# A two-layer decoder trunk on one core: all splits of the expert blocks on DVE, gathered tokens' pairs among the dense gates, 24 instead of 34 blocks in plain fp32

## The chip, the core and the metric

One core of a Trainium2 chip runs the whole step. Its engines are TensorE (PE, with its weight loads PEld), VectorE (DVE), ScalarE (ACT), GpSimd (POOL) and SyncE (SP, which here only issues DMAs). Each engine works through its own instructions strictly in order; semaphores tie the engines together. The metric is device microseconds of one execution, lower is better. A block below is one 128x1024 fp32 tile of an expert table, 512 KB.

## The reference

Each of the two layers runs a mixer (layer 0: gated linear attention and RG-LRU; layer 1: RWKV-7) and then PEER, a retrieval over 16384 one-neuron experts. The change lies in PEER alone:

```python
def block(xb):                       # 128 tokens
    q = normalised (xb @ w_q) per head
    s1, s2 = q[..., :128] @ keys0.T, q[..., 128:] @ keys1.T
    v1, i1 = lax.top_k(s1, 16); v2, i2 = lax.top_k(s2, 16)
    cand = v1[..., :, None] + v2[..., None, :]
    sc, pos = lax.top_k(cand.reshape(..., 256), 16)
    eidx = (i1 * 128 + i2) at pos
    gate = jax.nn.softmax(sc)
    act = jax.nn.gelu(u_tab[eidx] . xb)
    return sum(gate * act * v_tab[eidx])
```

There are 304 tokens: 16 learned ones, 256 of a prompt and 32 of samples.

## The kernel before

`peer` (L738) works in two ways. For 256 tokens it is **dense**: all 128 blocks of the table u go through PE (`up`), the gelu of each block is multiplied by a gate matrix that is zero except at the chosen experts (`weigh`, L1015), and all 128 blocks of v are accumulated into PSUM (`down`). The other tokens (48 in layer 0, 32 in layer 1) are **gathered**: POOL issues indirect DMAs for their rows of u and v (`rows`, L1073) and DVE does the dot products (`gup`, L1080) and the weighted sum (`gdown`, L1094). Layer 0 has 24 gathers of u and 24 of v, layer 1 has 16 and 16, each of two 512 KB DMAs, through three buffers `ab`.

Most blocks run as three fp32r products instead of one fp32 product, for which a block is **split**: ACT rounds raw into `wh` (L170), and DVE or POOL subtracts `wl = raw - wh` (L171). `wh` and `wl` have 3 buffers each, `raw` has 5. `u_pool` and `v_pool` (L202 and L203) say which blocks POOL subtracts: u blocks 34 to 59 and the odd ones above, every fifth v block below 100 and every second one from 100 on, 94 of 222 per layer. The first `nf` = 34 u blocks are not split; they run as plain fp32 (16 matmul instructions each) against `x32`.

The stages of one layer are: queries and top 16; `pairs(0)`, which ranks the 256 dense tokens' candidates; the **gate stage**, in which 32 calls of `ggroup` build the gate matrix (DVE writes one-hot tiles into the three buffers `ab`, PE multiplies them, ACT copies, SP writes 1 MB to the DRAM tensor `G` after every second call) while PE also runs the u blocks up to `ahead` = 36; then the **dense stage**, from the first `down` to the last, in which one v block and one u block alternate for 92 steps and v blocks alone follow for 36. Every eighth `weigh` loads 1 MB of `G` back into a `gb` buffer. `pairs(1)` and `gprep` rank the gathered tokens' candidates and work out their rows; the gathers start 100 units after `tp`.

The order is made by due times: `at(due, fn)` collects all units, they are traced in order of `due`, and a scheduler that goes by its own estimates then orders the instructions on each engine. `late` additionally keeps a unit's instructions behind the last marked instruction of the same engine. The units are estimated microseconds; `tw` is the due time of the first `down`, `tu` = 2.56 is one block.

Of the kernel before, what the change touches and what calls it, by code (L numbers as in the profile page):

```python
# [20 lines left out]
P = 128  # L21
# [147 lines left out]
def split(nc, src, h, l, eng=None):  # L169
    nc.scalar.activation(h, src, AF.Copy)  # L170
    return (eng or nc.vector).tensor_tensor(l, src, f(h), op=ALU.subtract)  # L171
# [10 lines left out]
class Prog:  # L182
    def __init__(self, tc, a, es):
        self.tc, self.nc, self.a, self.es = tc, tc.nc, a, es
        self.n, self.mark, self.turn, self.ready = 0, {}, {}, []
        self.extra(None, 0, 0)
        pool = lambda name, **kw: es.enter_context(tc.tile_pool(name=name, **kw))
        self.const = pool("const", bufs=1)
        self.strm = pool("strm", bufs=1)
        self.xp = pool("xp", bufs=1)  # L190
        self.ps = pool("ps", bufs=1, space=PSUM)
        k = self.const.tile([P, 4 * P], F32, name="k_all")
        self.k = k
        self.ident, self.o1024, self.o256, self.iota = (k[:, j * P:(j + 1) * P] for j in range(4))
        self.kdiag = self.const.tile([P, 48], F32, name="k_diag")
        pp = dict(ring=42, ahead=36, nf=34, lag=14, g2=-50, tq=10.0, ps=91.0, pl=42.0, gs=2.85, gl=14.0, u0=78.0, us1=3.5,
                  um=60, vm=5, te=25, vt=100, wu=0, wv=0, cl=0.01, us=2, gj=0.5)
        self.pp = pp
        self.mp = dict(q0=-3.6, q1=.12, p0=-3.0, p1=.14, a0=-2.2, a1=.14, i0=-1.45, i1=.2, c0=0, c1=.24, t0=1.5, t1=.15,
                       o0=.2774, o1=.1, f0=-1.0, f1=4.0, fe=.15, f2=7.9085, fl=.035)  # L200
        self.ring, self.lag, self.g2 = (pp[n] for n in ("ring", "lag", "g2"))
        self.u_pool = lambda e: e < pp["um"] or e % pp["us"] == 1  # L202
        self.v_pool = lambda e: e % (pp["vm"] if e < pp["vt"] else 2) == 0  # L203
        self.mhalf = self.const.tile([P, 6], F32, name="mhalf")
        self.nc.gpsimd.memset(self.mhalf, -0.5)
        self.vm1 = self.const.tile([P, 13, KB], F32, name="vm1")
        self.shf = self.const.tile([P, KB, 8], F32, name="shf")
        self.lnv = self.const.tile([P, 8, KB], F32, name="lnv")
# [529 lines left out]
    def peer(self, xh, xl, l):  # L738


        nc, a = self.nc, self.a
# [5 lines left out]
        with ExitStack() as es:  # L747
            pp = es.enter_context(self.tc.tile_pool(name=f"pe{l}", bufs=1, reuse_waits="tile"))
# [5 lines left out]
            gb = lambda shape, dt=F32: self.t(pr, shape, dt, "gb", 4)  # L754
            G = self.t(dp, [16, P, P, 16], F32, "G")
# [3 lines left out]
            at = lambda due, fn, *args: units.append((due, len(units), fn, args))  # L759

            def late(due, fn, *args):

                def queued():
                    with ExitStack() as q:
                        for ins in self.mark.values():
                            q.enter_context(self.tc.issue_after(getattr(ins, "ins", ins)))
                        fn(*args)
                at(due, queued)
# [171 lines left out]
            gs = [None]  # L940
# [24 lines left out]
            pp_ = self.pp  # L965
# [3 lines left out]

            wts = {}  # L970

            def up_load(e):
                if e < pp_["nf"]:
                    raw = self.stream("raw", F32)
                    nc.sync.dma_start(raw, a[f"ut{l}"][e])
                    wts["u", e] = raw, None
                    return
                wts["u", e] = self.wtile(a[f"ut{l}"][e], nc.gpsimd if self.u_pool(e) else None)

            def up(e):  # L980
                wh, wl = wts.pop(("u", e))
# [11 lines left out]
            gr, coef = [None], {}  # L993

            def down_load(e):
                hl = gb([P, 2, KB, P], F32R) if e == P - 1 else None
                wts["v", e] = self.wtile(a[f"v{l}"][e * P:(e + 1) * P, :].rearrange("p (k d) -> p k d", k=KB),
                                         nc.gpsimd if self.v_pool(e) else None, hl if hl is None else (hl[:, 0], hl[:, 1]))

            def weigh(e):  # L1000

                if e % 8 == 0:
                    gr[0] = gb([P, 16, 8, 16])
                    nc.sync.dma_start(gr[0].rearrange("p b i t -> p b (i t)"),
                                      G[:, :, e:e + 8, :].rearrange("b p i t -> p b (i t)"))
                if e >= P - NL:
                    ch, cl = (tl([P, 256], "act", NR, F32R) for _ in range(2))
                elif e % 2:
                    cc = tl([P, 2, 256], "qs", 3, F32R)
                    ch, cl = cc[:, 0, :], cc[:, 1, :]  # L1010
                else:
                    ch, cl = (tl([P, 256], "sc", 6, F32R) for _ in range(2))
                c = acts.pop(e)
                v16 = lambda ap: ap.rearrange("p (b t) -> p b t", t=16)
                self.mark[True] = nc.vector.tensor_tensor(v16(c), v16(c), gr[0][:, :, e % 8, :], op=ALU.mult)  # L1015
                split(nc, c, ch, cl)
                coef[e] = ch, cl
# [95 lines left out]
            tq, tu = pp_["tq"], 2.56  # L1113
# [8 lines left out]
            for h in range(8):  # L1122
                t, z = tq * h, h == 7
# [4 lines left out]
                b = t + (12.5 if z else 23.3)  # L1128
# [4 lines left out]
            ps = pp_["ps"]  # L1133
            at(ps, pairs_now, 0)
            tg = ps + pp_["pl"]
# [2 lines left out]
            for q in range(32):  # L1138
                at(tg + 1 + pp_["gs"] * q, ggroup, q)
            tw = tg + 1 + 32 * pp_["gs"] + pp_["gl"]  # L1140
            tp = tw + self.g2

            steps = pairs(1)
            for j in range(14):
                (at if j < 10 else late)(tw - pp_["gl"] + 0.5 + 0.8 * j if j < 10 else tp + 42 + 3 * j, lambda: steps.pop(0)())
            late(tp + 85, gprep)
            ahead, u0, u1 = pp_["ahead"], pp_["u0"], pp_["us1"]
            n0 = int((tg - u0) / u1)
            for e in range(P):
                if e < n0:  # L1150
                    tup = u0 + u1 * e
                elif e < ahead:
                    tup = tg + (tw - tg) * (e - n0 + 0.5) / (ahead - n0)
                else:
                    tup = tw + 2 * tu * (e - ahead) + 0.1
                tdn = tw + 2 * tu * e if e < P - ahead else tw + 2 * tu * (P - ahead) + tu * (e - P + ahead)
                at(tup - pp_["wu"], up_load, e)
                at(tup, up, e)
                at(tdn - (pp_["wv"] if e else 4.0), down_load, e)
                at(tdn - pp_["cl"], weigh, e)  # L1160
                at(tdn, down, e)
            gc = [(g, c) for g in range(len(groups)) for c in range(0, groups[g][1], 2)]
            t1 = tp + 100
            te = tw + 2 * tu * (P - ahead) + tu * ahead
            tg = (te - pp_["te"] - 15 - t1) / (2 * len(gc))
            for j, (g, c) in enumerate(gc):
# [626 lines left out]
```

## Time and profile before

| what | us |
| --- | --- |
| median of 3 runs | 2682.76 (2682.07 to 2689.53) |
| profiled execution | 2687.88 |
| its span, first to last instruction | 2686.1 |
| gate stage, layer 0, to the first `down` | 360 to 498 |
| dense stage, layer 0 | 498 to 1178 |
| dense stage, layer 1 | 1989 to 2650 |

The two dense stages are half of the span. PE is busy for 2478 us and its weight loads for 2259 us; POOL is busy for 1063 us, DVE for 1906 us. A busy PE is not yet PE at its pace: its granted clock has two levels (1.2 and 2.4 GHz), and the profile gives the mean of a stretch as a share of the higher one. Idle time of an engine counts only where another engine waits for it, so the way to read this profile is by stage: how long PE idles there, at which clock it works, and on whom it waits.

### The profile page before, as it was taken

The numbers are of one execution on the slowest core, as the hardware profiler recorded it, in microseconds if no ns is written. First come the engines' busy times: TensorE is split into PE (matmuls) and PEld (weight loads), VectorE is DVE, ScalarE is ACT, GpSimd is POOL, SyncE is SP. The second block draws the span as 40 slices with busy tenths as digits, with TensorE's granted clock in tenths as the row PEclk, the third lists the DMA queues.
The fourth block names the chain that finished last, engine by engine and source line by source line (L and its number), as shares of the span: only waits on it lengthen the run. The fifth ranks groups of instructions, "written<-read, shape, count | busy, mean of one in ns | idle before, by whom it ended". The sixth has DMA issues, their size and how long they took to land. (4 is left out here: it accounts for less than half of the span.)

```text
span 2686.1 us, 46850 instructions
## 1 busy us (share of the span) xinstructions
PE 2478.1 (92%) x18242; PEld 2258.7 (84%) x18242; DVE 1905.8 (71%) x4002; ACT 1146.9 (43%) x2072; POOL 1063.3 (40%) x836
## 2 busy tenths in 40 slices
PE   7999999989999999978999998899998899999996
PEld 6878889879999999977666656787997899999996
DVE  5455886568676888768587785589657766677776
ACT  7424233434444444434454452433343444444443
POOL 3335100356444454556333432520034534444444
PEclk9979999999999999988999999899999999999998
DMA  5323345687777988642211102324577767797772
GB/s 160 102 76 120 95 173 213 203 262 263 264 270 260 364 275 299 230 136 80 68 41 41 35 24 97 107 91 154 213 226 233 236 236 236 241 319 263 264 237 92
DMA packets 197895, 490.08 MB, mean 182 GB/s; under 512 B 21397, under 2 KB 91429, under 8 KB 192937
## 3 DMA queue, kind: packets, MB, share of 16 engines
q1 hardware_dynamic: 173480, 401.10, 45.7%
q0 software_dynamic: 23040, 83.90, 8.5%
q8 instruction: 143, 2.34, 0.4%
q10 hardware_dynamic: 1152, 2.10, 0.2%
q14 instruction: 80, 0.65, 0.1%
HBM read 447.41 MB, written 39.63 MB: 181 GB/s over the span
## 5 line engine op out<-in xcount | busy, mean ns | idle before, releaser
L171 POOL TENSOR_TENSOR wl<-raw,wh 128x1024 fp32r<-128x1024 f32 x240 | 615.1, 2565 | 1103.0 <-ACT wh L170 1055.0
L170 ACT ACTIVATE wh<-raw 128x1024 fp32r<-128x1024 f32 x519 | 549.0, 1059 | 813.2 <-PE ps_mm L162 362.5
L171 DVE TENSOR_TENSOR wl<-raw,wh 128x1024 fp32r<-128x1024 f32 x279 | 364.5, 1307 | 171.3 <-ACT wh L170 163.4
L162 PE MATMUL ps_u<-xh,wl 128*128 128x256 f32 x1504 | 427.0, 284 | 17.7 <-DVE wl L171 10.2
L162 PE MATMUL ps_u<-xh,wh 128*128 128x256 f32 x1504 | 428.5, 285 | 0.0
L162 PE MATMUL ps_u<-xl,wh 128*128 128x256 f32 x1504 | 425.3, 283 | 0.0
L162 PE MATMUL ps_mm<-qs,wh 128*128 128x256 f32 x1984 | 373.0, 288 | 0.0
L162 PE MATMUL ps_mm<-sc,wh 128*128 128x256 f32 x1984 | 358.3, 282 | 6.8 <-DVE sc L171 3.6
L162 PEld LDWEIGHTS ps_mm<-qs,wh 128*128 128x128 f32 x1984 | 315.7, 195 | 1.1 <-issue 0.8
L162 PE MATMUL ps_mm<-qs,wl 128*128 128x256 f32 x992 | 287.3, 290 | 31.6 <-DVE wl L171 31.6
L162 PEld LDWEIGHTS ps_mm<-sc,wh 128*128 128x128 f32 x1984 | 308.8, 193 | 8.2 <-DVE sc L171 4.2
L162 PEld LDWEIGHTS ps_u<-xh,wl 128*128 128x128 f32 x1504 | 287.2, 191 | 20.2 <-DVE wl L171 11.2
L162 PE MATMUL ps_mm<-sc,wl 128*128 128x256 f32 x992 | 279.9, 283 | 16.7 <-DVE wl L171 15.6
L162 PEld LDWEIGHTS ps_u<-xh,wh 128*128 128x128 f32 x1504 | 287.9, 191 | 0.1
L162 PEld LDWEIGHTS ps_u<-xl,wh 128*128 128x128 f32 x1504 | 287.5, 191 | 0.1
L1015 DVE TENSOR_TENSOR act<-act,gb 128x256 f32<-128x256 f32 x256 | 153.7, 642 | 114.0 <-DMA gb<-G 107.5
L162 PEld LDWEIGHTS ps_mm<-qs,wl 128*128 128x128 f32 x992 | 194.2, 196 | 34.8 <-DVE wl L171 34.0
L162 PEld LDWEIGHTS ps_mm<-sc,wl 128*128 128x128 f32 x992 | 191.3, 193 | 18.3 <-DVE wl L171 16.6
L171 DVE TENSOR_TENSOR sc<-act,sc 128x256 fp32r<-128x256 f32 x124 | 171.1, 1380 | 50.0 <-ACT sc L170 50.0
L990 ACT ACTIVATE act<-ps_u 128x256 f32<-128x256 f32 x256 | 94.8, 371 | 153.4 <-PE ps_u L162 153.4
L162 PE MATMUL ps_u<-wh,raw 128*128 128x256 f32 x544 | 140.1, 389 | 9.0 <-ACT act L990 9.0
L162 PE MATMUL ps_mm<-xh,wh 128*128 128x304 f32 x416 | 134.7, 327 | 8.6 <-ACT xh L344 4.2
(556 smaller groups left out, 4926.9 us busy)
## 6 DMA issues: line engine op xcount, KB each, us to landing
raw<-in_ut SPq DMA_DIRECT2D x256, 512.0 KB
raw<-in_v SPq DMA_DIRECT2D x256, 512.0 KB
G<-gb SPq DMA_DIRECT2D x32, 1024.0 KB
gb<-G SPq DMA_DIRECT2D x32, 1024.0 KB
raw<-in_wq SPq DMA_DIRECT2D x32, 512.0 KB
raw<-in_w_in SPq DMA_DIRECT2D x20, 512.0 KB
raw<-in_w_out SPq DMA_DIRECT2D x8, 512.0 KB
raw<-in_w_r SPq DMA_DIRECT2D x8, 512.0 KB
```

The costliest lines, as they stand in the source:

```text
L162: nc.tensor.matmul(out, lhsT, rhs, start=start, stop=stop, skip_group_check=True)
L170: nc.scalar.activation(h, src, AF.Copy)
L171: return (eng or nc.vector).tensor_tensor(l, src, f(h), op=ALU.subtract)
L990: nc.scalar.activation(acts[e], pu, AF.Gelu_apprx_tanh)
L1015: self.mark[True] = nc.vector.tensor_tensor(v16(c), v16(c), gr[0][:, :, e % 8, :], op=ALU.mult)
```

## The change

`u_pool` and `v_pool` are gone: `wtile` is called without an engine, and DVE subtracts all 104 split u blocks and 128 v blocks of each layer. `nf` falls from 34 to 24. The loads of `G` become a unit of their own, `gates_load`, due four blocks ahead of the `weigh` that needs them. `pairs(1)` and `gprep` are traced among the calls of `ggroup`, and no longer as `late` units in the dense stage. The gathers start 15 units after `tw` (before: 50 after it), and `lag`, from a gather to the arithmetic on it, is 20 instead of 14 units.

```diff
-        pp = dict(ring=42, ahead=36, nf=34, lag=14, g2=-50, tq=10.0, ps=91.0, pl=42.0, gs=2.85, gl=14.0, u0=78.0, us1=3.5,
-                  um=60, vm=5, te=25, vt=100, wu=0, wv=0, cl=0.01, us=2, gj=0.5)
+        pp = dict(ring=42, ahead=36, nf=24, lag=20, g2=15, tq=10.0, ps=91.0, pl=42.0, gs=2.85, gl=14.0, u0=78.0, us1=3.5,
+                  te=25, wu=0, wv=0, cl=0.01, gj=0.5)
-        self.u_pool = lambda e: e < pp["um"] or e % pp["us"] == 1
-        self.v_pool = lambda e: e % (pp["vm"] if e < pp["vt"] else 2) == 0
...
-                wts["u", e] = self.wtile(a[f"ut{l}"][e], nc.gpsimd if self.u_pool(e) else None)
+                wts["u", e] = self.wtile(a[f"ut{l}"][e])
...
-                                         nc.gpsimd if self.v_pool(e) else None, hl if hl is None else (hl[:, 0], hl[:, 1]))
+                                         None, hl if hl is None else (hl[:, 0], hl[:, 1]))
+            def gates_load(e):
+                gr.append(gb([P, 16, 8, 16]))
+                nc.sync.dma_start(gr[-1].rearrange("p b i t -> p b (i t)"),
+                                  G[:, :, e:e + 8, :].rearrange("b p i t -> p b (i t)"))
...
                 if e % 8 == 0:
-                    gr[0] = gb([P, 16, 8, 16])
-                    nc.sync.dma_start(gr[0].rearrange("p b i t -> p b (i t)"),
-                                      G[:, :, e:e + 8, :].rearrange("b p i t -> p b (i t)"))
+                    gr[0] = gr.pop(1)
...
-            tp = tw + self.g2
-            steps = pairs(1)
-            for j in range(14):
-                (at if j < 10 else late)(tw - pp_["gl"] + 0.5 + 0.8 * j if j < 10 else tp + 42 + 3 * j, lambda: steps.pop(0)())
-            late(tp + 85, gprep)
+            for j, step in enumerate(pairs(1)):
+                at(tg + 1.1 + pp_["gs"] * (8 + 1.5 * j), step)
+            at(tg + 1.1 + pp_["gs"] * 31, gprep)
...
+                if e % 8 == 0:
+                    at(tdn - (pp_["cl"] if e == 0 else 4 * tu), gates_load, e)
...
-            t1 = tp + 100
+            t1 = tw + pp_["g2"]
```

Three places show what this does to the order on the engines; all are in layer 0, and the lines of the changed kernel are its own. In the rows a tile's name is followed by its buffer's and its instruction's number.

DVE in the steady part of the dense stage, before: `wl` is a split, `qs` or `sc` a coefficient, `L1080` the arithmetic on a gathered row, which here waits for the DMA into `ab`.

```order
L171 TENSOR_TENSOR wl_1108_7280<-raw_1106_7277,wh_1107_7279 128x1024
L1080 SCALAR_TENSOR_TENSOR ab_1070_7029,ha1_766_4927<-ab_1070_7029,gb_745_4884 128x1024
L171 TENSOR_TENSOR qs_1152_7594<-act_795_5130,qs_1152_7594 128x256
L171 TENSOR_TENSOR wl_1115_7321<-raw_1113_7318,wh_1114_7320 128x1024
L1080 SCALAR_TENSOR_TENSOR ab_1090_7169,ha1_766_4927<-ab_1090_7169,gb_745_4884 128x1024
L171 TENSOR_TENSOR sc_1162_7663<-act_806_5201,sc_1161_7662 128x256
```

After, the same kind of place:

```order
L171 TENSOR_TENSOR wl_1218_8092<-raw_1216_8089,wh_1217_8091 128x1024
L171 TENSOR_TENSOR wl_1221_8122<-raw_1219_8119,wh_1220_8121 128x1024
L1083 SCALAR_TENSOR_TENSOR ab_1173_7800,ha1_699_4549<-ab_1173_7800,gb_678_4506 128x1024
L171 TENSOR_TENSOR sc_1265_8434<-act_910_5975,sc_1264_8433 128x256
L171 TENSOR_TENSOR wl_1228_8161<-raw_1226_8158,wh_1227_8160 128x1024
L171 TENSOR_TENSOR wl_1231_8191<-raw_1229_8188,wh_1230_8190 128x1024
```

DVE now has two splits per step where it had one or two.

POOL in the dense stage, before: splits, and between them the DMAs of the gathers (`L1073`).

```order
L171 TENSOR_TENSOR wl_914_5941<-raw_912_5938,wh_913_5940 128x1024
L1073 DMA ab_917_5972<-in_u0,er0_747_4886 128x1024 x2
L171 TENSOR_TENSOR wl_925_6013<-raw_923_6010,wh_924_6012 128x1024
L171 TENSOR_TENSOR wl_934_6081<-raw_932_6078,wh_933_6080 128x1024
L1073 DMA ab_937_6112<-in_u0,er0_747_4886 128x1024 x2
```

After, from the last instruction of the queries (`rs`, L830) on:

```order
L830 TENSOR_TENSOR rs_411_2695<-rs_411_2695,mhalf_69 48x1
L1076 DMA ab_749_4858<-in_u0,er0_680_4508 128x1024 x2
L1076 DMA ab_769_4996<-in_u0,er0_680_4508 128x1024 x2
L1076 DMA ab_799_5204<-in_u0,er0_680_4508 128x1024 x2
L1076 DMA ab_819_5344<-in_u0,er0_680_4508 128x1024 x2
```

Nothing but the gathers is left on POOL here, and the first of them stand behind no instruction of the gate or dense stage.

SP from the first load of the gate matrix (`gb<-G`) on, before: `raw` are blocks of u and v.

```order
L1004 DMA gb_667_4347<-G_247_1731 128x16x128
L251 DMA raw_699_4554<-in_v0 128x1024
L251 DMA raw_702_4584<-in_ut0 128x1024
L251 DMA raw_709_4622<-in_v0 128x1024
L251 DMA raw_712_4652<-in_ut0 128x1024
L251 DMA raw_718_4718<-in_v0 128x1024
L251 DMA raw_721_4748<-in_ut0 128x1024
L251 DMA raw_730_4795<-in_v0 128x1024
```

After:

```order
L1002 DMA gb_718_4655<-G_247_1731 128x16x128
L249 DMA raw_744_4825<-in_ut0 128x1024
L1002 DMA gb_784_5101<-G_247_1731 128x16x128
L249 DMA raw_751_4865<-in_v0 128x1024
L249 DMA raw_754_4895<-in_ut0 128x1024
L1002 DMA gb_865_5662<-G_247_1731 128x16x128
L249 DMA raw_761_4933<-in_v0 128x1024
L249 DMA raw_764_4963<-in_ut0 128x1024
L249 DMA raw_771_5003<-in_v0 128x1024
L1002 DMA gb_946_6224<-G_247_1731 128x16x128
```

Eight of the sixteen loads of the gate matrix now follow one another within the first 24 rows; before, one stood there, and seven more came within 17 rows, 17 rows later.

## Rows read from the trace of the kernel before

**Rows 1.** Page, part 1: busy us (share of the span) and instructions.
```profile
PE 2478.1 (92%) x18242; PEld 2258.7 (84%) x18242; DVE 1905.8 (71%) x4002; ACT 1146.9 (43%) x2072; POOL 1063.3 (40%) x836
```
**Rows 2.** Windows: length, busy us of PE, PEld, DVE, ACT, POOL; PEclk, DMA share, GB/s.
```profile
360.00:482.00 122.00, 120.11 (x787) 108.81 (x787) 78.89 (x131) 48.80 (x89) 5.62 (x2) 1.00 0.59 211
482.00:498.00 16.00, 14.37 (x106) 13.53 (x104) 0.75 (x3) 6.42 (x10) 7.19 (x3) 1.00 0.91 296
513.60:539.00 25.40, 21.20 (x158) 20.99 (x157) 24.66 (x47) 8.23 (x10) 10.78 (x5) 0.87 0.45 144
575.00:605.00 30.00, 24.54 (x194) 24.13 (x193) 23.46 (x34) 10.79 (x16) 15.17 (x10) 0.94 1.04 335
875.00:920.00 45.00, 40.16 (x323) 39.55 (x322) 38.56 (x56) 17.59 (x27) 26.39 (x13) 0.96 1.09 354
498.00:1178.00 680.00, 641.47 (x5221) 634.34 (x5221) 516.68 (x592) 296.53 (x444) 347.93 (x193) 0.96 0.78 264
1985.00:2650.00 665.00, 631.80 (x5205) 625.93 (x5204) 480.83 (x539) 295.89 (x441) 301.84 (x161) 0.98 0.74 245
```
**Rows 3.** Chain that ended last, pieces of layer 1: start us, us, what.
```profile
2377.65 4.28 PE ps_mm L162 x22
2396.61 2.78 PE ps_mm L162 x22
2555.00 75.92 PE ps_mm L162 x648
```
**Rows 4.** Waits, 500:1180, of PE and of DVE: us, times, longest us.
```profile
PE ps_mm L162 <- DVE wl L171: 25.8, 10, 4.4
...
DVE act L1015 <- DMA gb<-G: 29.4, 5, 13.6
```
**Rows 5.** DVE's groups by form, 498:1178: busy us, mean ns, idle before.
```profile
L171 DVE TENSOR_TENSOR sc<-act,sc 128x256 fp32r<-128x256 f32 x62 | 81.0, 1306 | 19.0 <-ACT sc L170 19.0
L1015 DVE TENSOR_TENSOR act<-act,gb 128x256 f32<-128x256 f32 x127 | 77.8, 654 | 31.2 <-DMA gb<-G 29.4 <-ACT act L990 1.8
L171 DVE TENSOR_TENSOR qs<-act,qs 128x256 fp32r<-128x256 f32 x62 | 52.9, 853 | 8.7 <-ACT qs L170 8.7
```
**Rows 6.** Lines L171 and L1015: ns min/median/max, first and last start.
```profile
L171 DVE TENSOR_TENSOR wl<-raw,wh x279: 1195/1225/3439, 13.0 to 2649.5; 128x1024 fp32r<-128x1024 f32 x140
L171 POOL TENSOR_TENSOR wl<-raw,wh x240: 2343/2398/8678, 14.4 to 2652.1; 128x1024 fp32r<-128x1024 f32 x120
L171 DVE TENSOR_TENSOR sc<-act,sc x124: 408/422/2622, 499.1 to 2638.4; 128x256 fp32r<-128x256 f32 x124
L171 DVE TENSOR_TENSOR qs<-act,qs x124: 408/419/4574, 499.4 to 2638.7; 128x256 fp32r<-128x256 f32 x124
...
L1015 DVE TENSOR_TENSOR act<-act,gb x256: 405/416/5601, 497.3 to 2640.1; 128x256 f32<-128x256 f32 x128
```
**Rows 7.** Timeline 703:719 of POOL and DVE: start us, us, [idle before <-releaser].
```profile
702.41 3.02 POOL L171 TENSOR_TENSOR wl<-raw,wh 128x1024 fp32r<-128x1024 f32 x1 [0.70 <-ACT wh L170]
703.10 2.61 DVE L171 TENSOR_TENSOR sc<-act,sc 128x256 fp32r<-128x256 f32 x1
...
713.27 1.23 DVE L1080 SCALAR_TENSOR_TENSOR ab<-ab,gb 128x1024 f32<-128x1024 f32 x1 [6.43 <-DMA ab<-in_u,er]
```
**Rows 8.** Timeline of the gate stage, 340:500: DVE, PE, SP.
```profile
408.88 0.69 DVE L950 TENSOR_TENSOR ab<-iota,iT 128x1024 f16<-128x1024 f16 x1 [2.32 <-PE ps_s L162]
...
480.62 2.05 PE L162 MATMUL ps_s<-ab 128*128 128x128 f16 x16
482.50 1.91 PE L162 MATMUL ps_u<-wh,raw 128*128 128x256 f32 x8
...
485.78 0.47 PE L162 MATMUL ps_u<-xh,wh 128*128 128x256 f32 x1
...
489.13 0.38 SPq L1004 DMA_DIRECT2D gb<-G  x1
...
497.25 0.76 DVE L1015 TENSOR_TENSOR act<-act,gb 128x256 f32<-128x256 f32 x2 [24.60 <-DMA gb<-G]
```

More of the change, by code (lines that the diff above doesn't have):

```diff
@@ L970, in peer @@
             wts = {}
+            fp32 = lambda e: e < pp_["nf"]
             def up_load(e):
-                if e < pp_["nf"]:
+                if fp32(e):
                     raw = self.stream("raw", F32)
```

## The prediction

> **What bounds the kernel now.** The page's busy line comes first [rows 1]: PE is busy for 92% of the span, twice as much as POOL or ACT, so a change pays where PE idles or runs at a low clock, and costs where it adds such time. The windows by stage are next [rows 2]. In the dense stage PE is busy for 641.47 of 680 us in layer 0 and for 631.80 of 665 in layer 1: it idles for 38.5 and 33.2 us. Its granted clock there is 0.96 and 0.98 on average, so 4% and 2% of the stretches, 27 and 13 us, were not granted; as part of that falls on idle time I count 30 of the 40. The two stages thus lose 72 + 30 = 102 us, and nothing else in the kernel is touched but the gate stage ahead of them, where PE is busy for 120.11 of 122 us.
>
> The pace without a loss is in the chain [rows 3]: 27 v blocks in 75.92 us, 2.81 a block. The chain also shows what a stall costs beyond itself: 22 matmuls of a block take 2.78 us, but 4.28 right behind a wait, at the lower of the two clocks.
>
> Whom PE waits for stands in its waits [rows 4]: most of all `wl` from DVE, 25.8 us in ten waits. But DVE has idle time in that stage, 163 of 680 us, so it is late and not full. Two things make it late. First, POOL: the coefficient subtraction `sc` takes 1306 ns on average and 422 in the median, `qs` 853 and 419, the gate product 654 and 416 [rows 5, 6]. The timeline shows why: POOL's split runs from 702.41 to 705.43, a DVE subtraction that starts within it lasts to 705.71, 2.61 us instead of 0.42 [rows 7]. Over the group counts that is 62 x 0.88 + 62 x 0.43 + 127 x 0.24 = 112 us of stretched DVE time in layer 0. Second, DMAs in DVE's in-order queue: 29.4 us for loads of the gate matrix [rows 4], and for gathers whose DMAs were issued late by a POOL in the middle of splits (6.43 us in one wait, [rows 7]); the splits queued behind stand still, and PE after them.
>
> **Part by part.** *Splits.* 94 leave POOL in each layer, at a median of 2.40 us, and 104 more come to DVE at 1.225 [rows 6]. In the dense stage DVE gets some 91 more, 111 us, and gives back the 112 of stretching: it stays at about 517 of 640 us, 81%. In a steady step DVE does two splits, a gate product, two coefficient subtractions' worth of work and about one gathered row (taken as 1.25, as the 1.23 of [rows 7]): 2.45 + 0.42 + 0.42 + 1.25 = 4.5 us against PE's 5.6; in the last 36 steps 1.23 + 0.84 + 0.6 = 2.7 against 2.81, close, but the durations overlap a little. Also a block needs ACT and one DVE split in a row where it needed ACT and POOL's 2.4 to 3: with three buffers of `wl` the split may start when PE ends the block three before, so the slack grows. POOL has nothing left but gathers, so a gather goes out when its buffer comes free, some 30 us before its arithmetic.
>
> *What stays late.* By the order, the loads of the gate matrix still come in two bursts, now eight within 24 rows of SP's queue at the start and seven later. DVE's gate products run up to 36 steps ahead of need and stand in front of splits. A load takes 489.13 to 497.25 = 8.1 us [rows 8]; two splits' worth of PE time, 5.6 us, lies between two loads. With two buffers free for them, each load is some 2.5 us late, over six loads 15, of which the slack takes half. Before, bursts cost 30 - 24.54 = 5.5 and 45 - 40.16 = 4.8 us of PE idle, with the DMA share at 1.04 and 1.09 [rows 2]. I take 7 for the first (it is longer, and gathers run beside it; ends 2 and 14), 5 for the second (0 to 8), 2 for the rest (0 to 6; 28 before), and 4 for the clock (1 to 10): 18 per layer, 36 in both. Gain: 102 - 36 = 66.
>
> *Gate stage.* A plain block takes 482.50 to 485.78 = 3.28 us of PE, a split one 2.81; nine of the ten lie ahead of the last `ggroup`: -4 us. Against it stands DVE. Its 131 instructions of the stage take 78.89 us, 0.60 each, 2.4 per call, and it idles for 2.32 us per two calls waiting for PE [rows 2, 8]: 43 us are free. Added are nine splits, 11 us, and `pairs(1)` with part of `gprep`: in 513.6 to 539 DVE was busy for 24.66 us with little else, 2.6 of it splits [rows 2], so 22 at most, and 11 at least, if POOL's 10.78 us stretched all it could; I take 15. But they fall on the last 19 calls: DVE 19 x 2.4 + 11 + 15 = 72 us, PE 19 x 1.88 + 9 x 2.81 + 3.3 = 64. The three buffers `ab` hold two calls, 4.8 us, as a store. Left: 3 us late (0 to 10). So the last call ends 1 us earlier (-4 to +6).
>
> *From there to the first down* no PE speed helps: G is written, read back, and lands 497.25 - (480.62 + 2.05) = 14.6 us after the last call's matmuls [rows 8]. Before, PE covered this with 3.5 to 4.5 u blocks and idled for 16 - 14.37 = 1.6 us [rows 2]. After, by the order, three blocks and the small matmuls of `gprep` are left, about 10 us. And POOL, with nothing queued ahead, issues three gathers (3 MB) as soon as `gprep` gives the rows, into a stretch where the DMAs have a share of 0.91 already [rows 2]: 3 MB at 296 GB/s would be 10 us if all of it went first, nothing if it went last. I take 5 (0 to 10). The first `down` comes 4 us later (-4 to +16 with the above), and I add 2 for the clock after so long a hole (0 to 3). By then PE has done 1.4 u blocks fewer than before (+4) and `gprep`'s matmuls more (-2). Per layer 4 + 2 + 2 = +8, in both +16.
>
> The Trainium skill, page "DMA: Bandwidth & Descriptors", section on queues, rings and completion order, says that a DMA engine goes round between the queues that have work, packet by packet; by that the read of G would get half of the engines while gathers are queued, and come 8 us later instead of 5, which would make the sum 6 us more. No row here shows that read beside gathers.
>
> *Sum.* -66 + 16 = -50. The profiled execution took 2687.88 us, 5.1 above the median of the runs; made against it, the changed kernel's profiled run would be 2638, and against the median 2682.76 it is **2633 us**.
>
> **Rivals.** *A: everything goes.* The gathers land behind the read of G, the bursts find enough slack, and the stages lose 4 us per layer: -94, gate stage and first down -3 per layer, +2 for u blocks: 2683 - 96 = 2587. For it: the steady order is regular, and the tail of layer 1 ran 27 blocks without a wait [rows 3] with POOL at work. Against it: 1.04 and 1.09 of DMA share in bursts [rows 2], and 8.1 us per load.
>
> *B: DVE bounds the gate stage.* `pairs(1)` and `gprep` cost 22, the store of two calls doesn't last, and the last call ends 9 us later than I take; in both layers +18, with 3 each for the clock +24: 2657. For it: 72 against 64 us in the last 19 calls. Against it: half of the 22 was POOL's stretching.
>
> *C: slower, by the gate matrix in DVE's queue.* All six or seven loads of each burst are late, and as DVE is the only one that splits, no POOL block bridges the wait, as 94 did before. From about 2.8 us per load on, over 13 loads, the stages lose what they lost before; at 4 us, as when 1 MB needs 10 us in a stretch that asks for 1 MB of G, 1 MB of blocks and part of a gather every 5.6 us (over 400 GB/s, where 354 is the most in the rows), it is 52 less 6 of slack, plus 6 for the clock: 52 per layer, -102 + 104 + 16 = +18: 2701. For it: the arithmetic. Against it: the bursts of before, almost as dense, cost 5 us each.
>
> *D: DVE is full.* The Trainium skill, page "Perfetto Trace Analysis", section on optimizing Scalar/DVE operations, says that work may be offloaded even to GPSIMD if DVE is saturated (and adds that it may not help, as the two share a port): taking it back would then cost. As a mechanism here: if the stretched times were DVE's own, the last 36 steps would need 1.3 + 0.65 + 1.1 + 0.6 = 3.65 us against 2.81, 30 per layer: 2633 + 60 = 2693. Rows 6 and 7 speak against it: the medians are the short times, and the long one ends with POOL's split.
>
> That nothing changes where it should is part of this: the ten blocks fewer in plain fp32 buy almost nothing in my sum, since the read of G sets the first `down`.
>
> **How the numbers follow.** The forecast has a chance of 0.54 (2633, own range 2612 to 2655), A 0.18 (2587), B 0.15 (2657), C 0.11 (2701), D 0.02 (2693). The range of 8 in 10 goes from 2596 to 2678: below it lies half of A's chance, above it C, D and little else. 0.3%, 8 us, is about what a measurement can tell here: faster means below 2675, slower above 2691. Faster: forecast, A and most of B, 0.85; same: the rest of B and the better end of C, 0.05; slower 0.10.
>
> **What would show it.** In the dense stage's DVE groups `sc`, `qs` and the gate product fall to about 0.42 us, and DVE is busy for about 500 to 520 us in each, with more splits; otherwise D. PE's idle there falls from 38.5 and 33.2 to about 14 per layer, left in two places, the two bursts, with waits of `act` on `gb<-G` ahead of them; if these are longer than 30 us per layer, C. Between the last `ggroup` and the first `down` PE has a hole of about 10 us; if it is short, the gathers didn't delay the read; if the last `ggroup` itself is late, B. Waits on gathers should be gone. I am wrong if PE's idle in the dense stage doesn't fall, or if it falls and the time doesn't.

## The result and the profile after

The changed kernel takes 2592.73 us (2583.4 to 2597.26) against 2682.41: a ratio of 0.9655 with an interval of 0.9623 to 0.9687. The forecast was 2633 us in a range of 2596 to 2678: the sign was right, but the gain was 90 us instead of 50, and the time lies 3 us below the range. The experiments ran on several chips, on which the kernel before took 2682 to 2698 us in the median, so ratios to the kernel before in the same rounds are compared, or stretches of the profiles.

The profiled execution has a span of 2595.2 us, 90.9 less than before. From marks that both traces have (the first `ggroup` matmul, the first `down`, the first of the last four v blocks, whose coefficients are in `act`):

| stretch | before | after | difference |
| --- | --- | --- | --- |
| first `ggroup` to first `down`, layer 0 | 134.8 | 138.8 | +4.0 |
| dense stage, layer 0 | 676.3 | 620.4 | -55.9 |
| first `ggroup` to first `down`, layer 1 | 133.8 | 139.8 | +6.0 |
| dense stage, layer 1 | 661.9 | 616.2 | -45.7 |

What is left, +0.7, lies outside the two PEER stages. The dense stages by these marks, before (length, busy us of PE, PEld, DVE, ACT, POOL, clock, DMA share, GB/s):

```profile
498.20:1174.50 676.30, 638.82 (x5205) 632.29 (x5206) 515.09 (x591) 295.27 (x442) 345.31 (x192) 0.96 0.78 264
1989.00:2650.90 661.90, 628.97 (x5180) 623.31 (x5181) 480.75 (x537) 294.32 (x439) 300.57 (x160) 0.98 0.74 244
```

and after, with the stretch from the last `ggroup` to the first `down` ahead of them:

```profile
482.70:504.00 21.30, 14.72 (x93) 11.36 (x90) 6.38 (x16) 6.81 (x13) 6.16 (x6) 0.95 1.01 352
...
503.90:1124.30 620.40, 618.61 (x5214) 617.82 (x5215) 465.26 (x625) 294.08 (x439) 120.45 (x98) 0.99 0.84 284
1944.00:2560.20 616.20, 612.75 (x5174) 611.93 (x5175) 426.46 (x575) 292.46 (x436) 90.64 (x66) 1.00 0.78 257
```

PE's idle in the dense stages fell from 37.5 + 32.9 to 1.8 + 3.4 us, and its busy time by 20 + 16 us for about the same matmuls, since the clock rose from 0.96 and 0.98 to 0.99 and 1.00. The price stands ahead of them: a hole of 6.6 us in layer 0 and of 6.4 in layer 1, in stretches with a DMA share of 1.01 and 1.02. What is left of PE's waits on splits, layer 0 and then layer 1 (us, times, longest):

```profile
PE ps_u L162 <- DVE wl L171: 0.8, 1, 0.8
...
PE ps_u L162 <- DVE wl L171: 3.4, 3, 1.8
```

The three of layer 1 stand in its two bursts of loads of G (at 1987, 2295 and 2324 us).

DVE's groups in layer 0's dense stage, after (busy us, mean ns, idle before), answer to [rows 5]:

```profile
L171 DVE TENSOR_TENSOR wl<-raw,wh 128x1024 fp32r<-128x1024 f32 x217 | 270.5, 1247 | 142.8 <-ACT wh L170 135.3
...
L1018 DVE TENSOR_TENSOR act<-act,gb 128x256 f32<-128x256 f32 x126 | 48.9, 419 | 7.9 <-DMA gb<-G 6.0 <-issue 2.0
L171 DVE TENSOR_TENSOR sc<-act,sc 128x256 fp32r<-128x256 f32 x62 | 26.0, 419 | 0.0
L171 DVE TENSOR_TENSOR qs<-act,qs 128x256 fp32r<-128x256 f32 x62 | 26.0, 419 | 0.0
```

The gate product and both coefficient subtractions are at 419 ns. Waits on gathers are gone, and the ones on loads of G have come down from 29.4 [rows 4] to 6.0 us, in layer 1 from 29.9 to 12.6. DVE now idles for 135.3 us because ACT has not rounded the next block, and before ACT rounds a block it waits most of all for PE's matmuls, which free its buffer (from the page, whole span):

```profile
L170 ACT ACTIVATE wh<-raw 128x1024 fp32r<-128x1024 f32 x539 | 570.9, 1060 | 777.4 <-PE ps_mm L162 332.2
```

So for much of the stage DVE stands as far ahead of PE as the buffers let it.

### The profile page after: what moved, and what is told of

It is laid out like the page before. It is cut to its first block, busy times and chain, and to the rows that moved or that the text cites. A ratio compares the mean times of both kernels' runs of the same rounds, so it can differ in the third digit from the quotient of the medians.

```text
span 2595.2 us, 47120 instructions
## 1 busy us (share of the span) xinstructions
PE 2437.2 (94%) x18393; PEld 2232.2 (86%) x18402; DVE 1860.5 (72%) x4210; ACT 1163.0 (45%) x2092; POOL 611.9 (24%) x648
## 4 chain that ended last, share of the span: by engine, by line
PE 75%; DVE 14%; ACT 3%; issue 3%; POOL 2%; DMA 2%; SPq 0%; POOLq 0%; ACTq 0%; DVEq 0%
PE ps_mm L162 34%; PE ps_u L162 24%; PE ps_s L162 8%; PE ps_iv L162 3%; PE ps_pj L162 3%; DMA gb<-G 2%; PE ps_ch L162 1%; PE ps_po L162 1%; ACT wh L170 1%; DMA raw<-in_ut 1%; DVE wl L171 1%; DVE sq L1352 1%; DVE ab L910 1%; DVE tx L1560 1%; POOL mixl L171 0%
## 5 line engine op out<-in xcount | busy, mean ns | idle before, releaser
L171 DVE TENSOR_TENSOR wl<-raw,wh 128x1024 fp32r<-128x1024 f32 x487 | 609.3, 1251 | 356.0 <-ACT wh L170 340.8
L162 PE MATMUL ps_u<-xh,wh 128*128 128x256 f32 x1664 | 472.6, 284 | 3.6 <-ACT act L990 2.6
L162 PE MATMUL ps_u<-xh,wl 128*128 128x256 f32 x1664 | 470.1, 282 | 4.2 <-DVE wl L171 4.2
L162 PE MATMUL ps_u<-xl,wh 128*128 128x256 f32 x1664 | 468.3, 281 | 0.0
L162 PEld LDWEIGHTS ps_u<-xh,wh 128*128 128x128 f32 x1664 | 315.5, 190 | 5.2 <-ACT act L990 3.0
L162 PEld LDWEIGHTS ps_u<-xh,wl 128*128 128x128 f32 x1664 | 314.9, 189 | 5.2 <-DVE wl L171 5.0
L162 PEld LDWEIGHTS ps_mm<-sc,wh 128*128 128x128 f32 x1984 | 304.1, 190 | 13.4 <-ACT sc L170 13.4
L1076 POOL DMA_INDIRECT ab<-in_u,er x80 | 79.6, 995 | 865.2 <-DVE ab L1083 481.3
L1076 POOL DMA_INDIRECT ab<-in_v,er x80 | 129.8, 1622 | 409.1 <-DVE gb L1097 325.5
L171 POOL TENSOR_TENSOR wl<-raw,wh 128x1024 fp32r<-128x1024 f32 x52 | 126.0, 2428 | 76.5 <-ACT wh L170 68.8
L162 PE MATMUL ps_mm<-xh,wh 128*128 128x304 f32 x416 | 135.3, 329 | 8.0 <-ACT xh L342 4.2
L162 PE MATMUL ps_s<-ab 128*128 128x128 f16 x1024 | 133.4, 296 | 1.7 <-ACT gb L959 1.3
```

The costliest lines, as they stand in the source:

```text
L162: nc.tensor.matmul(out, lhsT, rhs, start=start, stop=stop, skip_group_check=True)
L1076: nc.gpsimd.indirect_dma_start(out=w[:, j, :], out_offset=None, in_=a[f"{tab}{l}"], in_offset=bass.IndirectOffsetOnAxis(ap=gst[g][0][:, c ...
```

## Experiments

The dense stages of each kernel, by the same marks, carry the comparisons (us, layer 0 + layer 1; PE's idle in them beside):

| kernel | POOL splits | dense stages | PE idle | ratio to before |
| --- | --- | --- | --- | --- |
| before | yes | 676.3 + 661.9 = 1338 | 70 | 1 |
| e2: before, DVE splits all | no | 628.0 + 626.5 = 1255 | 14 | 0.969 (0.966 to 0.973) |
| e16: before, one gather | yes | 656.0 + 637.1 = 1293 | 38 | 0.979 (0.974 to 0.984) |
| e1: changed, POOL's splits back | yes | 647.7 + 627.6 = 1275 | 33 | 0.970 (0.967 to 0.974) |
| e6: e1, gathers later | yes | 654.1 + 640.3 = 1294 | 50 | 0.982 (0.976 to 0.988) |
| e11: e1, loads used 2.3 us later | yes | 678.0 + 661.2 = 1339 | 75 | 0.997 (0.995 to 1.000) |
| e15: e1, one gather | yes | 627.4 + 621.0 = 1248 | 17 | 0.964 (0.959 to 0.969) |
| changed | no | 620.4 + 616.2 = 1237 | 5 | 0.966 (0.962 to 0.969) |
| e4: changed, gathers later | no | 618.9 + 615.7 = 1235 | 6 | 0.965 (0.960 to 0.969) |
| e8: changed, loads used 2.3 us later | no | 616.1 + 614.7 = 1231 | 4 | 0.962 (0.955 to 0.968) |
| e10: changed, loads used 4.6 us later | no | 622.9 + 614.3 = 1237 | 6 | 0.968 (0.964 to 0.971) |
| e14: changed, one gather | no | 615.3 + 612.1 = 1227 | 1 | 0.957 (0.952 to 0.962) |

Each row of stretches is one execution. Without POOL's splits, executions of one kernel agree to some 4 us (the changed kernel once more, e12, has 1233). With them they scatter more: e16 took 2630 to 2646 us and its profiled execution was the longest, e1 took 2612 to 2620 and again the longest was profiled. So of two rows with POOL's splits, differences of 10 us or so mean little.

### Either half of the change alone: e1 and e2

```diff
-                wts["u", e] = self.wtile(a[f"ut{l}"][e])
+                wts["u", e] = self.wtile(a[f"ut{l}"][e], nc.gpsimd if self.u_pool(e) else None)
...
-                                         None, hl if hl is None else (hl[:, 0], hl[:, 1]))
+                                         nc.gpsimd if self.v_pool(e) else None, hl if hl is None else (hl[:, 0], hl[:, 1]))
```

> The changed kernel, but POOL again makes the splits that it made before (94 per layer); the other parts of the change stay. Theory P (what was lost before is the time in which POOL's splits and DVE's subtractions exclude each other): the two dense stages grow back by 85 to 100 us in all, to about 2680; the mean of sc returns from 0.42 to 0.9 us or more, and PE idles for 25 us or more in each dense stage. Rival M (the loss was DMA waits in DVE's queue, which the moved gathers and gate loads took away): at most 20 us come back, 2613 or less, with few waits on gathers. Between, near 2640: both have a share.

In e2, which starts from the kernel before, `u_pool` and `v_pool` are False for all blocks.

> The kernel before with one edit: DVE makes all splits; 34 plain blocks, the ranking of the gathered tokens, gathers and gate loads as before. P: 2683 minus 85 or so, 2585 to 2615, and PE's idle in each dense stage falls below 8 us. M: above 2655, with waits of DVE on DMAs of 25 us or more per layer as before.

Each half alone gives most of the gain: 63 us of the dense stages by the moves (e1), 84 by the splits (e2), 102 by both. So POOL's splits cost 84 us in the old arrangement and 39 in the new one. On one chip and in the same rounds the whole times say the same: before 2697.69, e1 2614.29, e2 2608.99, and 2594.21 with both (e3, below, which is the changed kernel but for the ten plain blocks). By its time e1 came near to theory M, e2 to theory P; so neither theory holds by itself. That the stretching alone is not the price is seen in e1's layer 0, 500 to 1130 us:

```profile
L171 DVE TENSOR_TENSOR sc<-act,sc 128x256 fp32r<-128x256 f32 x60 | 89.8, 1496 | 19.2 <-ACT sc L170 19.1
L1020 DVE TENSOR_TENSOR act<-act,gb 128x256 f32<-128x256 f32 x121 | 73.3, 638 | 16.2 <-DMA gb<-G 13.4 <-ACT act L992 2.7
L1085 DVE SCALAR_TENSOR_TENSOR ab<-ab,gb 128x1024 f32<-128x1024 f32 x48 | 64.6, 1346 | 31.8 <-DMA ab<-in_u,er 31.8
```

`sc` takes 1496 ns, more than in the kernel before (1306), and yet 29 us of this layer's dense stage are gone, 63 in both. The waits on gathers are as long as before (31.8 us, before 21.4 for u and 10.1 for v); those on loads of G fell from 29.4 to 13.4.

In whole time POOL's splits cost less in the new arrangement than the 39 us. POOL, held in splits, issues its first gather at 509 us and not at 487, behind the read of G, and e1's first `down` comes 6.4 and 7.9 us sooner than the changed kernel's.

### Do delays add up? e8, e10 and e11

```diff
                     gr[0] = gr.pop(1)
+                    for _ in range(1 if e else 0):
+                        nc.vector.tensor_tensor(gr[0], gr[0], gr[0], op=ALU.max)
```

In the added line DVE passes once more over a load, values unchanged, before it is first used. e8 has this in the changed kernel, e10 twice, e11 in e1.

> The changed kernel; ahead of the first gate product on each load of the gate matrix but the first, DVE passes over the load once more (one instruction on 128x2048, about 2.4 us, values unchanged). This is the 2.5 us by which the prediction had each load late, on all 15 loads of a layer. By the prediction's step, which let half of that reach PE: 15 x 1.2 = 18 us per layer, about 2629 (0.979). If the split blocks that stand ready cover such a delay whole: 2592 to 2600 (0.965 to 0.968), PE's idle in a dense stage at most 8 us.

> As e8, but DVE passes over each load twice (4.6 us of DVE for each of 15 loads, some with a split between the two). The blocks that stand split ahead are worth two blocks, 5.6 us of PE. If that is the slack, these 4.6 us still cost under 10 us in all (0.962 to 0.969); if the slack is nearer to 3 us, 1.5 us or more of each of the loads reach PE: 45 us or more, 0.98.

> e1 (POOL's splits back) with the pass over each load of e8, which cost nothing without POOL's splits. If delays add up in the same slack (the stretching by POOL has used it up), the pass costs here: 10 to 40 us more than e1, 0.974 to 0.985. If POOL's splits cost by a path of their own, it costs nothing here either: 0.967 to 0.973.

The pass took 2289 ns in the median in e8 and 2279 in e11 (2641 on average in layer 0, 2350 in layer 1). Without POOL's splits it costs nothing that can be measured, once or twice. With them the 30 passes of e11, 75 us of DVE in all, cost 64 us in the dense stages, more than the 10 to 40 expected: 42 of them are idle time of PE, 22 are longer busy time at a lower clock (0.96 and 0.98, in e1 0.98 and 0.99). In e8, layer 0:

```profile
498.40:1114.50 616.10, 614.41 (x5215) 613.60 (x5216) 495.61 (x640) 294.30 (x439) 161.58 (x98) 1.00 0.84 286
```

DVE is busy for 495.61 of 616.10 us, 80%, and PE idles for 1.7. In e1 DVE is busy for 78% and PE idles for 21.6; below it e11, with 79% and 40.8:

```profile
494.40:1142.10 647.70, 626.12 (x5219) 623.30 (x5218) 503.19 (x536) 293.91 (x438) 342.04 (x194) 0.98 0.82 277
...
494.60:1172.60 678.00, 637.17 (x5219) 633.11 (x5218) 535.40 (x551) 293.72 (x438) 364.24 (x194) 0.96 0.78 265
```

So DVE's busy share doesn't tell whether PE waits for it. Nor does its idle time for `wh`, which one might take for the slack. In layer 0 this is 135.3 us in the changed kernel, 109.9 in e8 and 82.1 in e10, with hardly any idle of PE in any of them. With POOL's splits it is 61.9 us before, 51.2 in e1, 55.5 in e11 and 59.9 in e15, while PE idles for 37.5, 21.6, 40.8 and 8.7. What tells it is a delay of known size put in on purpose, as here.

In e11 PE also waits for 12 us on POOL's own splits, in e1 for 0.2: the pass delays those too, since POOL is busy for 364 us in layer 0 instead of 342. How much of the 64 us came by that way was not separated.

### What uses up the slack: e4, e6, e14, e15, e16

e4 and e6 put the gathers' timing back, in the changed kernel and in e1:

```diff
-        pp = dict(ring=42, ahead=36, nf=24, lag=20, g2=15, tq=10.0, ps=91.0, pl=42.0, gs=2.85, gl=14.0, u0=78.0, us1=3.5,
+        pp = dict(ring=42, ahead=36, nf=24, lag=14, g2=50, tq=10.0, ps=91.0, pl=42.0, gs=2.85, gl=14.0, u0=78.0, us1=3.5,
...
```

> The changed kernel with the gathers' timing of before (start 50 after tw, lag 14), DVE making all splits. With POOL's splits the same step cost 19 us in the dense stages (e6 against e1). If delays only cost once the slack is used up, it costs nothing here, 0.962 to 0.968; if late gathers have a price of their own, 15 to 20 us, 0.971 to 0.973.

> The changed kernel with POOL's splits back as in e1, and besides the gathers' timing of the kernel before (start 50 after tw, lag 14). e1 was 0.970 of the kernel before, so with POOL's splits in place the other moves alone gave 3%. If the earlier gathers with more lag gave that, this goes back to 0.985 to 1.00; if it was the ranking of the gathered tokens that left the dense stage, it stays at 0.967 to 0.975.

The same step costs 19 us by the profiles with POOL's splits (by the ratios some 30, between e6's two expectations) and nothing without. But e4 is no test of the slack, because the delay doesn't arise in it: POOL, with nothing else queued, issues the first gathers at 486 us, as in the changed kernel, and DVE waits for no gather, while in e6 they go out at 553 and DVE waits for them for 33 us on u and 8 on v in layer 0. In e2, too, DVE waits for no gather, with the timing of before. So it is POOL's splits that make the gathers late, and that is part of their price. The delays that were tested against the slack are those of e8, e10 and e11.

In e14, e15 and e16 `rows` returns early when its table has one gather already, and `gup` and `gdown` work on that one: the other gathered rows are left out of the result, the instructions on DVE stay.

> The changed kernel with one gather from u and one from v in each layer instead of 40 pairs in all: the other gathers are left out, and DVE does all of its arithmetic on the one that is there (same instructions, same order). The dense stages were without a loss already, so the only gain should be the read of the gate matrix ahead of the first down, about as in e5: 2583 to 2594, 0.960 to 0.966.

> e1 (POOL's splits back) with the gathers left out as in e14. e1 against the changed kernel was 38 us in the dense stages. If the stretching of DVE by POOL's splits costs that by itself, this is still 25 to 40 us longer than e14 in the dense stages. If it takes the waits on late gathers besides (31.8 us in layer 0 of e1), it is within 10 us of e14.

> The kernel before with the gathers left out in the same way; POOL splits as before. The moves of the change gave 63 us of the dense stages while POOL split. If that was the gathers' waits, this comes near e1, 0.970 or less; if it was the ranking of the gathered tokens and the gate loads, it stays at 0.985 to 1.0.

With almost no gathers POOL's splits still cost 21 us (e15 against e14), with them 39: between the two expectations, about half each. e14 itself came out lower than expected, at 0.957: with nearly all of the gathers' traffic gone, the first `down` comes 4.1 and 3.5 us sooner than in the changed kernel, and the dense stages are 5.1 and 4.1 shorter. In e15 `sc` is stretched further still (500 to 1120 us), and PE idles for 17 us in the two layers together:

```profile
L171 DVE TENSOR_TENSOR sc<-act,sc 128x256 fp32r<-128x256 f32 x59 | 104.2, 1767 | 22.8 <-ACT sc L170 22.7
```

In the old arrangement the gathers were worth 45 of 1338 us (e16), between its two expectations; as e16's profiled execution was 12 us above its median, they may have been worth some 10 us more. The other 45 between e16 and e15 belong to what else moved, the ranking of the gathered tokens and the loads of G. These two were not separated, and that stays open; DVE's waits on G fell from 32.1 and 25.7 us in e16 to 7.6 and 11.7 in e15, its busy time by only 4 and 7 us, which points to the loads.

### The ten blocks, and the hole ahead of the first down: e3, e5, e13, e9, e7

```diff
-        pp = dict(ring=42, ahead=36, nf=24, lag=20, g2=15, tq=10.0, ps=91.0, pl=42.0, gs=2.85, gl=14.0, u0=78.0, us1=3.5,
+        pp = dict(ring=42, ahead=36, nf=34, lag=20, g2=15, tq=10.0, ps=91.0, pl=42.0, gs=2.85, gl=14.0, u0=78.0, us1=3.5,
...
```

> The changed kernel with 34 instead of 24 u blocks in plain fp32. If the prediction's step holds that the ten blocks buy almost nothing because the read of G sets the first down: 2590 to 2596. If PE's work counts wherever it lies, 20 blocks x 0.47 us = 9.4: about 2602, with the last ggroup or the end of the dense stage later by 4 to 5 us per layer.

2594.21 us, 0.964 (0.960 to 0.967): no difference. The first `down` came 1.9 and 3.8 us later, and the dense stages were 0.9 and 1.7 us shorter.

The hole in the changed kernel: the read of G is issued at 488.16 and used at 502.94, 14.8 us (DVE and SP; the last row is PE's):

```profile
488.16 0.38 SPq L1002 DMA_DIRECT2D gb<-G  x1
...
502.94 1.09 DVE L1018 TENSOR_TENSOR act<-act,gb 128x256 f32<-128x256 f32 x3 [5.21 <-DMA gb<-G]
...
503.86 1.44 PE L162 MATMUL ps_mm<-sc,wh 128*128 128x256 f32 x5 [6.57 <-ACT sc L170]
```

POOL's first six gather DMAs (three gathers) were issued from 486.65 to 493.15. e5 makes them wait for that read:

```diff
                 w = ab([P, 2, D])
+                if len(fetched) < 3:
+                    nc.gpsimd.tensor_copy(w[:, :, 0], gr[0][:, 0, 0, :2])
```

> The changed kernel, but the first three gathers of each layer wait until the first load of the gate matrix has landed (POOL copies two of its elements into the gathers' buffers first). If the 3 MB of gathers are what stretches that read from 8.1 to 14.7 us, the read takes 8 to 10 us again, PE's hole ahead of the first down falls from 6.6 to about 1.5 us, and both layers give 10 us: about 2583. If the stretching is something else, or the gathers then push the next loads back by as much: 2590 to 2596.

> e5 once more (gathers held until the gate matrix has been read). In e5 the first down came 5.7 and 6.6 us earlier and the dense stages grew by 3.4 and 1.7 us: if that is the whole effect, 6 to 8 us less than e12 on the same chip, 0.2 to 0.3%; if the 0.5% between e5 and the changed kernel was the chip's, no difference.

> The changed kernel once more, on the same chip and in the same rounds as e13: 0.962 to 0.969 of the kernel before.

In e5 the read is issued at 485.53, and POOL, which waits for it, copies at 491.99:

```profile
485.53 0.38 SPq L1002 DMA_DIRECT2D gb<-G  x1
...
491.99 0.44 POOL L1076 COPY ab<-gb 128x2 f32<-128x2 f32 x3 [193.14 <-PE ps_u L162]
```

The window from its last `ggroup` to its first `down`, with PE busy throughout:

```profile
479.60:495.00 15.40, 15.40 (x99) 12.05 (x97) 6.82 (x16) 7.36 (x14) 2.33 (x4) 1.00 0.88 274
```

That is 6.5 us instead of 14.8, and no hole: the gathers were its cause. The pair on one chip repeats it, 14.4 us in e12 and 6.2 in e13, where the profile names the read as what POOL's copy waited for; in layer 1 it is 15.3 us in both kernels with the gathers free, and 7.9 and 7.1 with them held. But the time hardly moves. e5 took 2587.13 (0.961, 0.957 to 0.964), e13 2592.59 beside e12's 2594.12 on one chip (0.9654 and 0.9658): no difference that can be measured. In e13 against e12 the first `down` comes 5.1 and 6.4 us sooner, and the dense stages are 3.1 and 5.2 us longer: held back, the gathers fall on the next loads of G. A later hold doesn't help either:

> e5 (gathers held until the gate matrix has been read) but held until the second load, and the gathers and their arithmetic 18 units later, so that the 3 MB fall less on the first loads. e5 had PE idle for 3 us in the 35 us behind its first down. If the gathers caused that, it goes below 1.5 us per layer and the time is 0.957 to 0.960; if the loads themselves did, as e5, 0.960 to 0.962.

2591.86 us, 0.963 (0.957 to 0.969); PE then waited 5.03 us in one place behind the first `down`. No complete version was found that is measurably faster than the changed kernel.

In e7, e1 with `lag=32`, the last weighted rows come behind the sum over them, so a part of the gathered result is left out.

> e1 with 32 instead of 20 units between a gather and the arithmetic on it. If POOL's splits now cost by issuing the gathers late (DVE waited 31.8 us on them in layer 0), these waits go, PE's idle of 21 us in layer 0 falls below 8, and the time comes to 0.962 to 0.965 of the kernel before. If they cost by the time in which they and DVE's subtractions exclude each other (sc at 1.5 us), it stays at 0.968 to 0.972.

It did neither: 0.984 (0.977 to 0.990), dense stages of 657.2 and 646.6 us. The waits on gathers stayed at 31.1 us in layer 0. POOL's gathers now waited for buffers on DVE's arithmetic, with splits queued behind them, and PE for POOL's splits (in layer 0 of e1 POOL waited so for 8.3 us, and PE not at all):

```profile
POOL ab L1078 <- DVE ab L1085: 91.0, 16, 8.8
...
PE ps_u L162 <- POOL wl L171: 16.7, 10, 3.3
```

## Why the prediction was right and wrong

*What bounds the kernel*: right in the place. It counted 72 us of idle and 30 of clock in the dense stages; 65 and 36 went. So the clock's 30 of 40 were too few. (Its example for the clock, 4.28 us "at the lower of the two clocks", is read too simply: the granted clock of that stretch is 0.62 on average, so it was at either level for a part.)

*Splits*: right that the stretched times would go (419 ns). DVE's busy time was forecast at 500 to 520 us in each stage and is 465 and 426. The step set the added splits against the stretching of three groups alone, and left out that the ranking and `gprep` leave this stage and that splits and row arithmetic were stretched a little, too. It also took layer 0's sum for layer 1, where DVE had been busy for 481 us and not 515.

*What stays late* is the step that failed, and with it the size. It kept 18 us per layer: 7 and 5 for the bursts of gate loads, 2 for the rest, 4 for the clock. Idle was 1.8 and 3.4. The bursts did come, but "each load is some 2.5 us late, over six loads 15, of which the slack takes half" was wrong in both parts. DVE waited on G for 6.0 us in all of layer 0 and 12.6 in all of layer 1, and of that 0.8 and at most 3.4 reached PE. And e8, which makes each load 2.3 us later in use, and e10, 4.6, show that the slack takes it all. The terms had been read from bursts of the kernel before, 5.5 and 4.8 us of idle, where POOL's splits and the gathers that they made late had used the slack up; e11 shows that with POOL's splits most of a delay does reach PE. Idle was thus mis-sized by 23 us (28 forecast in both layers, 5 left), and the clock by some 14 (22 of the counted 30 forecast as regained; PE's busy time fell by 36).

*Gate stage and first down*: right in the sum. The first `down` was forecast 4 us later and came 4.0 and 6.0 later; the last `ggroup` was to end 1 us earlier, and its matmuls came 2.2 and 1.2 us earlier (116.8 and 117.8 us behind the first, before 119.0 in both). The hole was forecast at about 10 us and was 6.6 and 6.4. The read of G was forecast 5 us later by the gathers; issue to use rose by 6.7 in layer 0, and e5 shows that they were the cause. That the ten plain blocks buy almost nothing was right (e3).

By the rule of the Trainium skill, page "DMA: Bandwidth & Descriptors", section on queues, rings and completion order, the prediction had 8 us instead of 5. The 6.7 us against the kernel before lie between the two, and the 8.3 us against e5 come close to the 8; so the traces agree with the rule but don't decide for it.

*Rivals*: A's dense stages (4 us of loss per layer) are what happened, but not its gate stages, forecast 3 us shorter, measured 4 and 6 longer. With A's one half and the forecast's other, -94 + 8 + 4 for u blocks, the sum would have been near 2600. B, C and D fell: the last `ggroup` wasn't late, the bursts cost PE under 4 us per layer, and DVE's subtractions took their short times. The range ended 3 us above the time, since it held only half of A's chance, and that the two halves could come apart wasn't weighed.

## What to carry to other kernels

Delays of an engine that works ahead through buffers don't add up one by one: here they cost nothing up to the slack (30 delays of 2.3 us in e8, 30 of 4.6 in e10), and most of their time where something else had used it up (64 of 75 us in e11). So a stall's price read from a congested kernel can't be carried over to one in which another source of delay is gone. Neither the busy share of the engine nor its idle time told how much slack was left; a delay of known size, put in on purpose, did. And the gain of two edits that feed the same slack is not the sum of theirs: 63 and 84 gave 102.

## What the runs showed of the hardware

I had not expected that three gathers (3 MB), issued from 1.5 us before a 1 MB read to 5 us after it, more than double that read: 14.8 instead of 6.5 us, in layer 1 15.3 instead of 7.9. With two gathers beside it (e14, 2 MB) it took 10.2 and 12.5. Behind the hole of 6.6 us PE's first matmuls took 415 to 583 ns instead of 276, but the clock cost little beyond them: it was 0.93 in the first 36 us and 1.00 in the next 30. And POOL's splits, whose conflict with DVE's subtractions made `sc` three to four times as long (419 ns without, 1306 before, 1767 in e15), cost PE 21 us in 1248 when little else was late.
